# Experts' rows added to the tokens' in DRAM by accumulating scatters

## The chip, the cores and the metric

The kernel runs as one program on one core of a Trainium2 chip. The metric is device time in microseconds, from the start to the end of an execution; lower is better. The engines are named as the profile names them: PE (TensorE, matmul), DVE (VectorE), ACT (ScalarE), POOL (GpSimd, which here also issues the indirect transfers) and SP (SyncE, which issues nearly all loads).

## What is computed

The reference runs two blocks of a network of two layers each over 512 tokens of 1024 numbers. The first block has token mixers and a convolutional feed-forward; the second has token mixing and a mixture of 16 experts. The change is in the mixture of experts. Each token goes to two experts; their results, weighted by gates, are added, and the layer norm takes the sum with the scaled input:

```python
def run_block(args):
    e, toks = args
    xb = x_pad[toks]
    h = jax.nn.silu(xb @ w1[e]) * (xb @ w3[e])
    return h @ w2[e]

yb = lax.map(run_block, (blk_e, slot_tok.reshape(n_blk, MOE_BLOCK)))
y = yb.reshape(-1, D) * slot_gate[:, None]
return jnp.zeros((N + 1, D), x2.dtype).at[slot_tok].add(y)[:N]
...
ffn = moe(x.reshape(B * S, D), w_router, router_bias, w1[l], w3[l], w2[l]).reshape(B, S, D)
x = layer_norm_2(DN_ALPHA_2 * x + ffn, ln2_g[l], ln2_b[l])
```

All is float32. The kernel makes a float32 product of three faster ones: an operand is split into a high and a low part, and hi·hi, lo·hi and hi·lo are added (`mm3`, lines 368 to 370).

## The kernel before

`moe` (called once per layer, about 1810 to 2153 us and 2630 us to the end) first routes: `idx[0]`, the tile `slots`, holds for each expert 96 places (`SLOTS`), in each the row of the token that goes there; a place without a token holds a row beyond the tensor's end and is dropped by the bounds check. `idx[1]`, the tile `slotw`, holds the gates. The token rows lie in DRAM as `xd`. For each expert POOL gathers its rows (`gather`, L1763, `AHEAD` = 4 experts in advance), PE transposes them, `turn` splits them (tile `Txt`), `up` makes 48 matmuls with the weights `wmoeu` (PSUM tile `HP`, result `Ha`), and `down` transposes that, splits it (`Yhi` on ACT, `Ylo` on DVE) and makes two half products c = 0 and 1 of 12 matmuls each with `wmoed` (PSUM tile `YP`). ACT scales the result by the gate into the tile `y` (L1829), and POOL scatters `y` (L1834). The product of expert e - 1 is made beside `up` of expert e; the last expert's, 15, comes after the loop, in the tail.

Before the change the scatters go to `yd`, which has 1024 rows: a token's first expert writes to row t and its second to row 512 + t, so that no row is written twice and the scatters need not wait for each other (the no-dependence group `rows{l}`). The rows of the last expert are set to zero first (`zero`, L1870, and one scatter), since its result never goes to DRAM. In the tail each of the four 128-token parts of h has two loads from `yd` (L1904, into staging tiles `wide`) and two adds, each cut in two halves: columns 0 to 511 on POOL (L1920), the rest on DVE (L1922). The last expert's rows are added on PE: `parts` makes two pieces of the gated result (`both`, L1909 on ACT and L1910 on DVE), and `stats` multiplies them by the one-hot tiles `own` (L1893), after h itself by the identity (L1933, L1935), so that the sum stands in PSUM for the layer norm.

Weights come in pairs of units, 1 MB a load, on SP's queue (`Stream.next`, L2072), into a ring of 6 `wide` tiles and 7 `g8` tiles. In the tail `ds_.apart` makes the splits go to `g8` tiles of their own. `y`, `own`, `zero` and other raw loads share a pool of three 4 KB tiles (`raw`).

Each engine works off its instructions in an order that the framework's scheduler sets before the run; SP's and POOL's queues are in order too, so a transfer that waits holds up those behind it. After layer 0's product PE goes on with the memory branch of the next layer (`memory_whole`, L1495 and L1504), after layer 1's with the final layer norm alone.

Of the kernel before, what the change touches and what calls it, by code (L numbers as in the profile page):

```python
# [21 lines left out]
S = 512  # L22
D = 1024
NT = 4
EPS = 1e-5
ALPHA = math.sqrt(2.0)
# [3 lines left out]
NE = 16  # L30
# [4 lines left out]
SLOTS = 96  # L35
# [253 lines left out]
class Net:  # L289
# [896 lines left out]
    def block2_consts(self):  # L1186
        nc = self.nc
        with self.phase("c2"):
            L = Lane(self, "L", w=8)
            self.tri, self.one_r = (self.blk.tile([128, 128], FR, name=n) for n in ("tri_r", "one_r"))  # L1190
            raw = L.w((128, 128))
            nc.sync.dma_start(raw, self.A["tri"])
            nc.vector.tensor_copy(self.tri, raw)
            nc.vector.tensor_copy(self.one_r, self.ones)
            self.iota = self.const("iota", 128, self.blk)
            self.rcnt = self.const("rcnt", 64, self.blk)
            self.wr = self.const("wr", 128, self.blk)
# [19 lines left out]
            self.yd = self.dram.tile([2 * S, D], F32, name="yd")  # L1217

    def rotary(self, L, ps, bias):

# [523 lines left out]
    def slots(self, L, T, n):  # L1744

        ve = self.nc.vector
        out = self.pp.tile([SLOTS, 2, n], I32, name=self.nm("slots"), tag="slot%d" % n, bufs=1)
        none, second, d = (L.s([SLOTS, n]) for _ in range(3))
        ve.tensor_scalar(none, T, 0.0, 65536.0, op0=OP.is_equal, op1=OP.mult)
        ve.tensor_scalar(second, T, 512.5, -512.0, op0=OP.is_gt, op1=OP.mult)  # L1750
        ve.scalar_tensor_tensor(d, T, -1.0, none, op0=OP.add, op1=OP.add)
        ve.tensor_tensor(out=out[:, 1], in0=d, in1=second, op=OP.add)
        self.placed = ve.tensor_copy(out[:, 0], d)
        return out

    def weights(self, T, n):
# [4 lines left out]
    def gather(self, xg, idx, e):  # L1761

        self.nc.gpsimd.indirect_dma_start(out=xg, out_offset=None, in_=self.xd,  # L1763
                                          in_offset=bass.IndirectOffsetOnAxis(ap=idx[0][:, 1, e:e + 1], axis=0),
                                          bounds_check=S - 1, oob_is_err=False)

    def turn(self, L, xg, raw=False):
# [58 lines left out]
    def rows(self, L, unit, a, idx, e, group=None):  # L1826
# [3 lines left out]
        self.scatter(y, idx, e, group)  # L1830

    def scatter(self, y, idx, e, group=None):

        put = self.nc.gpsimd.indirect_dma_start(out=self.yd,  # L1834
                                           out_offset=bass.IndirectOffsetOnAxis(ap=idx[0][:, 0, e:e + 1], axis=0),
                                           in_=y, in_offset=None, bounds_check=2 * S - 1, oob_is_err=False)
        if group:
            self.tc.declare_no_dep(put.ins, group=group, reason="each pair is one expert's")
            self.tc.add_to_no_dep_group(group, put.ins)

    def moe(self, l, lg, last):
        nc = self.nc
# [5 lines left out]
        def staging():  # L1848
            return self.wide.tile([128, 2, D], F32, tag="wide", bufs=WIDE, name=self.nm("wide"))
# [14 lines left out]
        idx, info = self.route(L, H, l, lg)  # L1864

        self.gather(xg[0], idx, 0)
        self.overflow(L, (T, H, Y), l, info)

        zero = self.rawp.tile([128, D], F32, tag="raw", name=self.nm("zero"))[0:SLOTS]
        with self.tc.issue_after(nc.gpsimd.memset(zero, 0.0).ins):  # L1870
            for e in range(1, AHEAD):
                self.gather(xg[e], idx, e)
            self.scatter(zero, idx, NE - 1, f"rows{l}")
        xt, a = self.turn(T, xg[0]), None
        down = lambda: self.rows(Y, ds_.next, a, idx, e - 1, f"rows{l}")
        unit = lambda: first.pop(0) if first else us.next()
        for e in range(NE):
            nxt = self.up(H, unit, xt, *((down,) if e == NE - 1 else ()))
            if e + 1 < NE:
                xt = self.turn(T, xg[(e + 1) % AHEAD])  # L1880
            if e + AHEAD < NE:
                self.gather(xg[e % AHEAD], idx, e + AHEAD)
            if 0 < e < NE - 1:
                down()
            if 4 <= e < 8:
                with self.tc.issue_after(self.turned.ins):
                    ac.activation(self.h[e - 4], self.h[e - 4], AF.Copy, scale=ALPHA)
            a = nxt
        own = self.rawp.tile([128, NT, 256], FR, tag="raw", name=self.nm("own"))[0:SLOTS, :, 0:128]
        tok = L.s([SLOTS, 1])  # L1890
        ve.tensor_copy(tok, idx[0][:, 1, NE - 1:NE])
        for t in range(NT):
            ve.tensor_scalar(own[:, t], self.iota[0:SLOTS], tok, -128.0 * t, op0=OP.subtract, op1=OP.is_equal)  # L1893
        ds_.apart = True
        last_units = [ds_.next() for _ in range(4)]
        cut = self.cut
        keys = values = None
        if not last:
            keys = self.memory_fetch(l + 1, 0)
        yys = []  # L1900
        for t in range(NT):
            yy = staging()
            for j in range(2):
                nc.sync.dma_start(yy[:, j], self.yd[j * S + t * 128:j * S + (t + 1) * 128, :])  # L1904
            yys.append(yy)
        both = self.g8(FR, (128, 2, D))[0:SLOTS]

        def parts(cs, ps, g):
            ac.activation(both[:, 0, cs], ps, AF.Copy, scale=g)  # L1909
            self.added = ve.scalar_tensor_tensor(both[:, 1, cs], ps, g, both[:, 0, cs].bitcast(F32), op0=OP.mult, op1=OP.subtract)  # L1910

        self.down(Y, iter(last_units).__next__, a, idx, NE - 1, parts)
        product = self.product
        gb = self.ln_rows(6 + 2 * l)
        self.hd = self.dram.tile([S, D], F32, name=self.nm("hd"))
        x = None if last else self.new_x()
        def add(t, after=None):
            z = self.h[t]
            for j in range(2):
                nc.gpsimd.tensor_tensor(out=z[:, 0:512], in0=z[:, 0:512], in1=yys[t][:, j, 0:512], op=OP.add)  # L1920
                with self.tc.issue_after(after.ins) if after else nullcontext():
                    ve.tensor_tensor(out=z[:, 512:D], in0=z[:, 512:D], in1=yys[t][:, j, 512:D], op=OP.add)  # L1922

        rest = staging().rearrange("p a (b c) -> p (a b) c", b=2)
        slots = itertools.count()
        H.w = lambda: rest[:, next(slots) % 4]
# [9 lines left out]
                sums.append(ps)  # L1936
            return self.ln_stats(H, sums)

        add(0, cut)
        add(1, cut)  # L1940
        add(2, self.added)
        fill = iter(())
        if not last:
            self.kv = self.g8()
# [1 line left out]
        with self.tc.issue_after(product.ins):  # L1946
            next(fill, None)
            now = stats(0)
        add(3, self.known_x)
# [11 lines left out]
    def overflow(self, L, lanes, l, info):  # L1961


        nc = self.nc
        ve = nc.vector
        E, g, r, xs, xe, ctr, n = info
        with self.tc.For_i(0, n, 1):
# [43 lines left out]
            self.scatter(y[0], idx, 0, f"rows{l}")  # L2011
            ve.tensor_scalar(ctr, ctr, 1.0, None, op0=OP.add)

    def run(self, upto=99):
# [109 lines left out]
```

## Time and profile before

| | |
|---|---|
| median of 3 runs | 2973.24 us (2969.78 to 2973.51) |
| the profiled execution | 2971.21 us |
| its span | 2969.3 us, so 1.9 us lie around it |
| PE busy | 2864.6 us (96%) |
| DVE busy | 2164.5 us (73%) |
| ACT busy | 1424.0 us (48%) |
| POOL busy | 463.2 us (16%) |
| mean DMA rate | 154 GB/s |

Busy shares are means over stages with different limits. The stage of the change is read by itself: by busy times in a stretch, by the waits of an engine, and in the tails by the timeline, which shows in the order of time what an engine did and what ended its idle time. In a row of the timeline `[1.21 <-DVE Ha L1799]` means 1.21 us idle before it, ended by that instruction. A transfer's time is told as from its issue to its landing.

### The profile page before, as it was taken

To read this page: it belongs to the slowest core of one execution; us is meant where nothing else is said; L and a number is where in the kernel's file an instruction comes from. 1 tells how busy PE (TensorE), PEld (TensorE's weight loads), DVE (VectorE), ACT (ScalarE), POOL (GpSimd) and SP (SyncE) were. 2 spreads that over 40 slices of the span, in tenths; PEclk is the share of its full clock that TensorE was granted. 3 is DMA by queue.
4 is the path that set the end of the run, shared out by engine and by line. 5 is a ranking of instruction groups with operands and counts; after the bars stand their busy time and mean duration, and the time that the engine had idled before them with its cause. 6 is when DMAs were issued, how large, how long until landed. Compare 5 with 4: busy or idle time off the path is not lost.

```text
span 2969.3 us, 37938 instructions
## 1 busy us (share of the span) xinstructions
PE 2864.6 (96%) x13982; PEld 2242.9 (76%) x13982; DVE 2164.5 (73%) x3460; ACT 1424.0 (48%) x2202; POOL 463.2 (16%) x443
## 2 busy tenths in 40 slices
PE   7999999999999999999999998999999999989996
PEld 6777888878678888888777786777687777867774
DVE  6988655665977556677876447999768754479997
ACT  4435433334344333435544424888445444238884
POOL 3412000014221000011101103120412011021203
PEclk9999999999999999999999998999999999989998
DMA  5131333333122333344232266999632322569993
GB/s 193 36 107 37 100 100 96 96 129 95 50 72 76 103 93 101 112 145 125 61 96 82 82 235 237 380 388 367 226 98 61 98 80 82 219 241 370 389 379 123
DMA packets 128589, 457.33 MB, mean 154 GB/s; under 512 B 15696, under 2 KB 16912, under 8 KB 126992
## 3 DMA queue, kind: packets, MB, share of 16 engines
q1 hardware_dynamic: 117776, 425.50, 41.6%
q0 software_dynamic: 7168, 16.79, 1.7%
q10 hardware_dynamic: 3456, 12.58, 1.1%
q8 instruction: 111, 1.82, 0.3%
q14 instruction: 78, 0.64, 0.1%
HBM read 429.12 MB, written 27.26 MB: 154 GB/s over the span
## 4 chain that ended last, share of the span: by engine, by line
PE 66%; DVE 7%; ACT 1%; issue 1%; POOL 1%; DMA 0%; POOLq 0%; DVEq 0%; ACTq 0%
PE AP L368 12%; PE AP L369 12%; PE AP L370 12%; PE HP L370 4%; PE HP L369 4%; PE HP L368 4%; PE YP L370 2%; PE YP L369 2%; PE YP L368 2%; PE BP L370 1%; PE BP L368 1%; PE BP L369 1%; DVE cacc L784 1%; PE O L1610 1%; DVE lo L376 1%
## 5 line engine op out<-in xcount | busy, mean ns | idle before, releaser
L368 PE MATMUL AP<-g,hi 128*128 128x512 f32 (+1 forms) x1856 | 718.1, 388 | 14.1 <-ACT Mw L711 4.0
L369 PE MATMUL AP<-g,hi 128*128 128x512 f32 (+1 forms) x1856 | 711.9, 384 | 8.1 <-DVE g L376 8.1
L370 PE MATMUL AP<-g,lo 128*128 128x512 f32 (+1 forms) x1856 | 712.4, 384 | 0.0
L376 DVE TENSOR_TENSOR lo<-raw,hi 128x1024 fp32r<-128x1024 f32 x314 | 400.2, 1276 | 363.2 <-ACT hi L374 354.2
L374 ACT CAST hi<-raw 128x1024 fp32r<-128x1024 f32 x326 | 341.6, 1050 | 575.6 <-PE AP L369 382.9
L368 PEld LDWEIGHTS AP<-g,hi 128*128 128x128 f32 x1856 | 353.0, 190 | 86.2 <-ACT Mw L711 4.4
L369 PEld LDWEIGHTS AP<-g,hi 128*128 128x128 f32 x1856 | 353.7, 191 | 75.3 <-DVE g L376 9.2
L370 PEld LDWEIGHTS AP<-g,lo 128*128 128x128 f32 x1856 | 353.2, 190 | 67.2 <-issue 2.6
L376 DVE TENSOR_TENSOR lo<-g,hi 128x1024 fp32r<-128x1024 f32 x204 | 239.2, 1219 | 23.4 <-ACT hi L374 23.0
L374 ACT CAST hi<-g 128x1024 fp32r<-128x1024 f32 x204 | 207.0, 1051 | 50.2 <-PE AP L370 32.4
L376 DVE TENSOR_TENSOR lo<-wide,hi 128x1024 fp32r<-128x1024 f32 x180 | 212.4, 1226 | 25.4 <-ACT hi L374 25.2
L370 PE MATMUL HP<-hi,Txt 128*96 128x512 f32 x512 | 203.9, 398 | 0.0
L369 PE MATMUL HP<-lo,Txt 128*96 128x512 f32 x512 | 203.3, 397 | 0.2
L368 PE MATMUL HP<-hi,Txt 128*96 128x512 f32 x512 | 201.0, 400 | 1.1 <-ACT Txt L374 1.1
L374 ACT CAST hi<-wide 128x1024 fp32r<-128x1024 f32 x180 | 182.7, 1050 | 22.2 <-PE HP L370 19.1
L368 PE MATMUL AP<-hi,g 128*128 128x512 f32 x400 | 165.0, 416 | 0.3 <-DVE g L886 0.3
L370 PE MATMUL AP<-hi,g 128*128 128x512 f32 x400 | 157.8, 397 | 0.2 <-DVE g L891 0.2
L369 PE MATMUL AP<-lo,g 128*128 128x512 f32 x400 | 156.8, 393 | 0.0
L368 PE MATMUL BP<-hi,g 128*128 128x512 f32 x352 | 136.8, 390 | 0.0
L369 PE MATMUL BP<-lo,g 128*128 128x512 f32 x352 | 136.6, 389 | 0.0
L370 PE MATMUL BP<-hi,g 128*128 128x512 f32 x352 | 134.1, 389 | 0.0
L384 POOL TENSOR_TENSOR Bs<-Bs,mhalf 128x1 f32<-128x1 f32 x8 | 7.8, 977 | 687.2 <-DVE Bs L383 687.2
(511 smaller groups left out, 5059.1 us busy)
## 6 DMA issues: line engine op xcount, KB each, us to landing
wide<-in_wmoeu SPq DMA_DIRECT2D x64, 1024.0 KB, 7.9
g<-in_wmoeu SPq DMA_DIRECT2D x64, 1024.0 KB, 8.4
raw<-in_wup SPq DMA_DIRECT2D x88, 512.0 KB, 3.5
g<-in_wmoed SPq DMA_DIRECT2D x34, 1024.0 KB, 8.7
wide<-in_wmoed SPq DMA_DIRECT2D x30, 1024.0 KB, 7.9
raw<-in_xwin SPq DMA_DIRECT2D x50, 512.0 KB, 3.6
raw<-in_xgate SPq DMA_DIRECT2D x48, 512.0 KB, 3.6
raw<-in_wdown SPq DMA_DIRECT2D x44, 512.0 KB, 3.5
```

What stands on the lines that cost most here:

```text
L368: mm(ps, a[0], b[0], start=start, stop=False)
L369: mm(ps, a[0], b[1], start=False, stop=False)
L370: self.product = mm(ps, a[1], b[0], start=False, stop=stop)
L374: self.nc.scalar.copy(hi, src)
L376: self.cut = (engine or self.nc.vector).tensor_tensor(out=lo, in0=src, in1=hi.bitcast(F32), op=OP.subtract)
L384: self.nc.gpsimd.tensor_tensor(out=r, in0=x, in1=self.mhalf[:, 0:n], op=OP.pow)
L784: ve.scalar_tensor_tensor(acc, ubs[c][:, j:j + S], w_dw[:, 31 * c + j:31 * c + j + 1], acc, op0=OP.mult, op1=OP.add)
L1610: nc.tensor.matmul(O[j][64 * b:64 * b + 64, t * 128:(t + 1) * 128], v[:, s, c:c + 64], PT[i - 1 + b][:, s, :], start=s == 0, stop=s == t, ...
```

## The change

`yd` is gone. Each layer has a tensor `sums` of 512 rows in DRAM, which starts as the scaled h, and the scatters of experts 0 to 14 add to it in DRAM. Since they go to the same rows, the framework has each wait for the one before. The tail loads four parts from `sums` straight into new h tiles, and no adds are left. The `slots` tile keeps one row number a place instead of two. The scaling of h moves from experts 4 to 7 to before the overflow loop (which runs zero times here), with four writes to `sums` on ACT's queue; `own` moves from the tail to just after that loop. Of the last expert's four weight units, two are split in advance and two when `down` asks for them. The order of POOL's adds and their places (`cut`, `added`) go with the adds.

```diff
     def slots(self, L, T, n):
...
-        ve.tensor_tensor(out=out[:, 1], in0=d, in1=second, op=OP.add)
-        self.placed = ve.tensor_copy(out[:, 0], d)
+        ve.tensor_tensor(out=out, in0=d, in1=second, op=OP.add)
...
+    def scatter(self, y, idx, e):
+
+        self.nc.gpsimd.indirect_dma_start(out=self.sums,
+                                          out_offset=bass.IndirectOffsetOnAxis(ap=idx[0][:, e:e + 1], axis=0),
+                                          in_=y, in_offset=None, bounds_check=S - 1, oob_is_err=False,
+                                          compute_op=OP.add)
...
         self.gather(xg[0], idx, 0)
+
+        self.sums = self.dram.tile([S, D], F32, name=self.nm("sums"))
+        for t in range(NT):
+            ac.activation(self.h[t], self.h[t], AF.Copy, scale=ALPHA)
+            ac.dma_start(out=self.sums[t * 128:(t + 1) * 128, :], in_=self.h[t])
+        mark = info[5]
         self.overflow(L, (T, H, Y), l, info)
-
-        zero = self.rawp.tile([128, D], F32, tag="raw", name=self.nm("zero"))[0:SLOTS]
-        with self.tc.issue_after(nc.gpsimd.memset(zero, 0.0).ins):
+        with self.tc.issue_after(nc.gpsimd.memset(mark, 0.0).ins):
             for e in range(1, AHEAD):
                 self.gather(xg[e], idx, e)
-            self.scatter(zero, idx, NE - 1, f"rows{l}")
+
+        own = self.pp.tile([SLOTS, NT, 128], FR, tag="own", bufs=1, name=self.nm("own"))
...
-            if 4 <= e < 8:
-                with self.tc.issue_after(self.turned.ins):
-                    ac.activation(self.h[e - 4], self.h[e - 4], AF.Copy, scale=ALPHA)
             a = nxt
-        own = self.rawp.tile([128, NT, 256], FR, tag="raw", name=self.nm("own"))[0:SLOTS, :, 0:128]
...
         ds_.apart = True
-        last_units = [ds_.next() for _ in range(4)]
-        cut = self.cut
+        last_units = [ds_.next() for _ in range(2)]
         keys = values = None
         if not last:
             keys = self.memory_fetch(l + 1, 0)
-        yys = []
+        self.new_h()
         for t in range(NT):
-            yy = staging()
-            for j in range(2):
-                nc.sync.dma_start(yy[:, j], self.yd[j * S + t * 128:j * S + (t + 1) * 128, :])
-            yys.append(yy)
+            nc.sync.dma_start(self.h[t], self.sums[t * 128:(t + 1) * 128, :])
...
-        self.down(Y, iter(last_units).__next__, a, idx, NE - 1, parts)
+        self.down(Y, lambda: last_units.pop(0) if last_units else ds_.next(), a, idx, NE - 1, parts)
...
-        def add(t, after=None):
-            z = self.h[t]
-            for j in range(2):
-                nc.gpsimd.tensor_tensor(out=z[:, 0:512], in0=z[:, 0:512], in1=yys[t][:, j, 0:512], op=OP.add)
-                with self.tc.issue_after(after.ins) if after else nullcontext():
-                    ve.tensor_tensor(out=z[:, 512:D], in0=z[:, 512:D], in1=yys[t][:, j, 512:D], op=OP.add)
```

What this does to the order of the instructions is shown at four places. SP's queue in the tail of layer 1 before: the last loads of weights, the loads of `yd`, the layer norm's rows (in brackets the semaphores that an instruction waits on; DMASW counts POOL's transfers, DMAHW those of SP and ACT).

```order
L2072 DMA wide_25390<-in_wmoeu 128x2x1024 [waits DMAHW5_49,DVE_49]
L2072 DMA wide_25423<-in_wmoed 128x2x1024 [waits DMAHW6_49,DVE_49]
L2072 DMA wide_25431<-in_wmoed 128x2x1024 [waits DMAHW7_49,DVE_49]
L1904 DMA wide_25439<-yd 128x1024 [waits DMAHW0_49,DMASW3_49,DVE_49]
L1904 DMA wide_25439<-yd 128x1024 [waits DMAHW1_49]
```

The same place after; between the two pairs of `in_wmoed` stand the four loads of `sums`.

```order
L2054 DMA wide_25372<-in_wmoeu 128x2x1024 [waits DMAHW1_49,DVE_49]
L2054 DMA wide_25398<-in_wmoed 128x2x1024 [waits DMAHW2_49,DVE_49]
L1898 DMA g_25406<-sums_22535 128x1024 [waits DMAHW3_49,DMASW1_49]
L1898 DMA g_25406<-sums_22535 128x1024 [waits DMAHW4_49]
L1898 DMA g_25407<-sums_22535 128x1024 [waits DMAHW5_49,DMASW7_49,PE_49]
L1898 DMA g_25407<-sums_22535 128x1024 [waits DMAHW6_49]
L2054 DMA wide_25438<-in_wmoed 128x2x1024 [waits DMAHW7_49,DVE_49]
```

The first load of `sums` waits on DMASW1, the last scatter's landing; the second pair has moved behind it. DVE before, at the end of the last `up` of layer 1 (`Ha` is its result, `lo` are splits in the ring, `g` splits of the last expert's units):

```order
L376 TENSOR_TENSOR lo_25403<-wide_25390,hi_25402 128x1024
L376 TENSOR_TENSOR g_25425<-wide_25423,g_25425 128x1024
L376 TENSOR_TENSOR g_25428<-wide_25423,g_25428 128x1024
L1799 TENSOR_TENSOR Ha_25412<-HP_25262,Ha_25412 96x512
L376 TENSOR_TENSOR g_25433<-wide_25431,g_25433 128x1024
L1893 TENSOR_SCALAR own_25416<-c_iota,Ls_5398_25417 96x128 x4
L376 TENSOR_TENSOR g_25436<-wide_25431,g_25436 128x1024
L1816 SCALAR_TENSOR_TENSOR Ylo_25458<-YP_25452,Yhi_25457 128x384
L1922 TENSOR_TENSOR g_21914<-g_21914,wide_25439 128x512 x2
```

DVE after, at the same place:

```order
L376 TENSOR_TENSOR lo_25375<-wide_25372,hi_25374 128x1024
L376 TENSOR_TENSOR lo_25385<-wide_25372,hi_25384 128x1024
L1797 TENSOR_TENSOR Ha_25394<-HP_25244,Ha_25394 96x512
L1814 SCALAR_TENSOR_TENSOR Ylo_25419<-YP_25413,Yhi_25418 128x384
L1903 SCALAR_TENSOR_TENSOR g_25412<-YP_25422,slotw_22525,g_25412 96x512
```

Nothing stands between `Ha` and `Ylo` any more: the early pair is split further ahead, the late pair after `parts` of the first half, and `own` at the stage's start. PE in the tail of layer 1 after, where the second half product (`YP_25437`) begins; before, its twelve matmuls stood in a row behind the first half's, and the statistics (L1933, L1935) behind those.

```order
L370 MATMUL YP_25422<-g_25403,Ylo_25419 96x512
L368 MATMUL YP_25437<-g_25440,Yhi_25418 96x512
L1919 MATMUL YP_25508<-g_25407,c_ident 128x512
L1921 MATMUL YP_25508<-g_25412,own_22738 128x512 x2
L1919 MATMUL YP_25512<-g_25407,c_ident 128x512
L369 MATMUL YP_25437<-g_25440,Yhi_25418 96x512
```

Four matmuls of the statistics of part 2 have moved between the first matmul of the second half, which waits for ACT's cast `g_25440` of the late pair, and the second, which waits for its split on DVE. ACT after, in the last two `up` of layer 1 (`y_24842`, `y_25012` and `y_25182` are the rows of experts 11, 12 and 13):

```order
L374 CAST hi_25205<-g_25193 128x1024
L1827 ACTIVATE y_24842<-YP_24852,slotw_22525 96x512
L1827 ACTIVATE y_24842<-YP_24876,slotw_22525 96x512
L374 CAST hi_25219<-g_25217 128x1024
L374 CAST hi_25229<-g_25217 128x1024
L1813 ACTIVATE Yhi_25188<-YP_25183 128x384
L374 CAST g_25400<-wide_25398 128x1024
L374 CAST g_25403<-wide_25398 128x1024
L374 CAST hi_25247<-g_25245 128x1024
L1827 ACTIVATE y_25012<-YP_25022,slotw_22525 96x512
L1827 ACTIVATE y_25012<-YP_25046,slotw_22525 96x512
L374 CAST hi_25257<-g_25245 128x1024
```

And ACT before, where the casts of the same weights stand (`hi_25223` there is `hi_25205` here), with the rows of expert 13 alone:

```order
L374 CAST hi_25223<-g_25211 128x1024
L374 CAST Txt_25185<-TP_25186 128x384
L374 CAST Txt_25185<-TP_25193 128x384
L374 CAST hi_25237<-g_25235 128x1024
L374 CAST hi_25247<-g_25235 128x1024
L1829 ACTIVATE y_25200<-YP_25210,slotw_22550 96x512
L374 CAST hi_25265<-g_25263 128x1024
```

The rows of experts 11 and 12 were made 36 and 18 us ahead of those of 13 before; they have moved to just ahead of them. POOL's order is not shown: it has the gathers and scatters in nearly their old sequence (some gathers one place earlier), each scatter with a further wait on a DMASW semaphore, and the 8 adds of each tail are gone.

## Rows read from the trace of the kernel before

**Rows 1.** Busy time by stretch: us, PE, PEld, DVE, ACT, POOL, clock, DMA, GB/s.

```profile
1860.00:2072.00 212.00, 212.00 (x1008) 150.86 (x1007) 196.90 (x204) 181.03 (x221) 29.40 (x20) 1.00 1.01 381
...
1824.00:1828.00 4.00, 4.00 (x14) 2.65 (x13) 1.11 (x2) 1.44 (x3) 3.04 (x4) 0.55 0.92 356
...
2116.00:2153.00 37.00, 37.00 (x124) 23.07 (x122) 28.49 (x42) 10.10 (x15) 20.42 (x17) 1.00 0.66 233
2929.00:2937.00 8.00, 6.69 (x17) 4.25 (x18) 6.54 (x11) 0.76 (x2) 7.38 (x4) 0.57 1.00 388
```

**Rows 2.** Waits of SP's queue, 1820 to 2106: us in total, times, longest.

```profile
SPq L2072 <- DVE lo L376: 211.4, 80, 7.7
```

**Rows 3.** Timeline of POOL, layer 1's tail: start, us, what [idle before].

```profile
2922.02 0.91 POOL L1834 DMA_INDIRECT yd<-y,slots  x1 [9.77 <-ACT y L1829]
```

**Rows 4.** Timeline of SP's queue, layer 1's tail.

```profile
2889.84 2.86 SPq L2072 DMA_DIRECT2D wide<-in_wmoed  x2
2925.69 4.58 SPq L1904 DMA_DIRECT2D wide<-yd  x8
```

**Rows 5.** Timeline of PE, layer 1's tail.

```profile
2928.00 0.55 PE L1808 MATMUL YP<-c_ident,Ha 96*128 96x96 f32 x4 [1.21 <-DVE Ha L1799]
2929.13 0.47 PE L368 MATMUL YP<-g,Yhi 128*96 128x512 f32 x1 [0.58 <-ACT Yhi L1815]
...
2931.52 0.74 PE L370 MATMUL YP<-g,Ylo 128*96 128x512 f32 x1 [1.18 <-DVE Ylo L1816]
...
2936.75 0.48 PE L369 MATMUL YP<-g,Yhi 128*96 128x512 f32 x1
...
2938.46 0.39 PE L370 MATMUL YP<-g,Ylo 128*96 128x512 f32 x1
2938.69 1.02 PE L1933 MATMUL HP<-g,c_ident 128*128 128x512 f32 x2
```

**Rows 6.** Timeline of DVE, layer 1's tail.

```profile
2927.26 0.68 DVE L1799 TENSOR_TENSOR Ha<-HP,Ha 96x512 f32<-96x512 f32 x1
2927.87 1.21 DVE L376 TENSOR_TENSOR g<-wide,g 128x1024 fp32r<-128x1024 f32 x1
2929.00 0.86 DVE L1893 TENSOR_SCALAR own<-c_iota,Ls 96x128 fp32r<-96x128 f32 x4
...
2930.92 0.55 DVE L1816 SCALAR_TENSOR_TENSOR Ylo<-YP,Yhi 128x384 fp32r<-128x384 f32 x1
```

**Rows 7.** Timeline of POOL, layer 0's tail.

```profile
2100.64 0.91 POOL L1834 DMA_INDIRECT yd<-y,slots  x1 [9.76 <-ACT y L1829]
2107.88 13.33 POOL L1920 TENSOR_TENSOR g<-g,wide 128x512 f32<-128x512 f32 x8 [6.33 <-DMA wide<-yd]
```

**Rows 8.** Timeline of all engines, first statistics of layer 1's tail.

```profile
2944.82 0.64 DVE L1922 TENSOR_TENSOR g<-g,wide 128x512 f32<-128x512 f32 x1
...
2945.60 1.02 POOL L384 TENSOR_TENSOR Hs<-Hs,mhalf 128x1 f32<-128x1 f32 x1 [0.81 <-DVE Hs L383]
```

**Rows 9.** Timeline of ACT at the start of layer 0's stage.

```profile
1824.07 0.48 ACT L374 CAST Txt<-TP 128x384 fp32r<-128x384 f32 x1 [16.00 <-PE TP L1774]
```

**Rows 10.** Line 1834, all scatters of the trace: issue to landing.

```profile
DMA to landing us min/median/max: 3.6/7.5/9.0
```

**Rows 11.** Waits at the start of layer 0's stage, 1806 to 1826.

```profile
POOL zero L1870 <- DMA g<-xd,slots: 4.0, 1, 4.0
```

**Rows 12.** DMA issues on the page: count, KB each, us to landing.

```profile
wide<-in_wmoed SPq DMA_DIRECT2D x30, 1024.0 KB, 7.9
```

**Rows 13.** DMA issues, 2885 to 2969.

```profile
wide<-in_wmoed SPq DMA_DIRECT2D x2, 1024.0 KB, 6.8
...
g<-in_ln_rows SPq DMA_DIRECT2D x1, 1024.0 KB, 11.1
```

**Rows 14.** Timeline of PE, layer 0's last product, around its middle.

```profile
2112.30 0.63 PE L370 MATMUL YP<-g,Ylo 128*96 128x512 f32 x2
```

**Rows 15.** Timeline of ACT, expert 13's first half, layer 1.

```profile
2906.32 0.68 ACT L1829 ACTIVATE y<-YP,slotw 96x512 f32<-96x512 f32 x1
```

More of the change, by code (lines that the diff above doesn't have):

```diff
@@ L1216, in block2_consts @@
             self.xd = self.dram.tile([S, D], F32, name="xd")
-            self.yd = self.dram.tile([2 * S, D], F32, name="yd")
     def rotary(self, L, ps, bias):
@@ L1746, in slots @@
         ve = self.nc.vector
-        out = self.pp.tile([SLOTS, 2, n], I32, name=self.nm("slots"), tag="slot%d" % n, bufs=1)
+        out = self.pp.tile([SLOTS, n], I32, name=self.nm("slots"), tag="slot%d" % n, bufs=1)
         none, second, d = (L.s([SLOTS, n]) for _ in range(3))
@@ L1763, in gather @@
         self.nc.gpsimd.indirect_dma_start(out=xg, out_offset=None, in_=self.xd,
-                                          in_offset=bass.IndirectOffsetOnAxis(ap=idx[0][:, 1, e:e + 1], axis=0),
+                                          in_offset=bass.IndirectOffsetOnAxis(ap=idx[0][:, e:e + 1], axis=0),
                                           bounds_check=S - 1, oob_is_err=False)
@@ L1824, in down, with rows @@
             out(slice(c * 512, c * 512 + 512), ps, idx[1][:, e:e + 1])
-    def rows(self, L, unit, a, idx, e, group=None):
+    def rows(self, L, unit, a, idx, e):
         y = self.rawp.tile([128, D], F32, tag="raw", name=self.nm("y"))[0:SLOTS]
         self.down(L, unit, a, idx, e, lambda cs, ps, g: self.nc.scalar.activation(y[:, cs], ps, AF.Copy, scale=g))
[L1830 to L1839, printed above, removed]
+        self.scatter(y, idx, e)
+    def scatter(self, y, idx, e):
[3 more added lines that the diff above has]
+                                          compute_op=OP.add)
     def moe(self, l, lg, last):
@@ L1866, in moe @@
         self.gather(xg[0], idx, 0)
+        self.sums = self.dram.tile([S, D], F32, name=self.nm("sums"))
[3 more added lines that the diff above has]
+        mark = info[5]
         self.overflow(L, (T, H, Y), l, info)
-        zero = self.rawp.tile([128, D], F32, tag="raw", name=self.nm("zero"))[0:SLOTS]
-        with self.tc.issue_after(nc.gpsimd.memset(zero, 0.0).ins):
+        with self.tc.issue_after(nc.gpsimd.memset(mark, 0.0).ins):
             for e in range(1, AHEAD):
                 self.gather(xg[e], idx, e)
-            self.scatter(zero, idx, NE - 1, f"rows{l}")
+        own = self.pp.tile([SLOTS, NT, 128], FR, tag="own", bufs=1, name=self.nm("own"))
+        tok = L.s([SLOTS, 1])
+        ve.tensor_copy(tok, idx[0][:, NE - 1:NE])
+        for t in range(NT):
+            ve.tensor_scalar(own[:, t], self.iota[0:SLOTS], tok, -128.0 * t, op0=OP.subtract, op1=OP.is_equal)
         xt, a = self.turn(T, xg[0]), None
-        down = lambda: self.rows(Y, ds_.next, a, idx, e - 1, f"rows{l}")
+        down = lambda: self.rows(Y, ds_.next, a, idx, e - 1)
         unit = lambda: first.pop(0) if first else us.next()
@@ L1884, in moe @@
                 down()
-            if 4 <= e < 8:
-                with self.tc.issue_after(self.turned.ins):
-                    ac.activation(self.h[e - 4], self.h[e - 4], AF.Copy, scale=ALPHA)
             a = nxt
-        own = self.rawp.tile([128, NT, 256], FR, tag="raw", name=self.nm("own"))[0:SLOTS, :, 0:128]
[L1890 to L1893, printed above, removed]
         ds_.apart = True
-        last_units = [ds_.next() for _ in range(4)]
-        cut = self.cut
+        last_units = [ds_.next() for _ in range(2)]
         keys = values = None
@@ L1909, in parts @@
             ac.activation(both[:, 0, cs], ps, AF.Copy, scale=g)
-            self.added = ve.scalar_tensor_tensor(both[:, 1, cs], ps, g, both[:, 0, cs].bitcast(F32), op0=OP.mult, op1=OP.subtract)
-        self.down(Y, iter(last_units).__next__, a, idx, NE - 1, parts)
+            ve.scalar_tensor_tensor(both[:, 1, cs], ps, g, both[:, 0, cs].bitcast(F32), op0=OP.mult, op1=OP.subtract)
+        self.down(Y, lambda: last_units.pop(0) if last_units else ds_.next(), a, idx, NE - 1, parts)
         product = self.product
@@ L1937, in stats @@
             return self.ln_stats(H, sums)
-        add(0, cut)
-        add(1, cut)
-        add(2, self.added)
         fill = iter(())
@@ L1948, in moe @@
             now = stats(0)
-        add(3, self.known_x)
         for t in range(NT):
@@ L2010, in overflow @@
             self.down(Y, lambda: (ds_.raw(),), a, idx, 0, out, True)
-            self.scatter(y[0], idx, 0, f"rows{l}")
+            self.scatter(y[0], idx, 0)
             ve.tensor_scalar(ctr, ctr, 1.0, None, op0=OP.add)
```

## The prediction, made before the changed kernel was timed

> **What bounds the kernel now.** I began with the busy times by stretch. In [rows 1] PE is busy for all of 212 us of layer 0's expert loop, DVE for 197 and ACT for 181 of them. The 1008 matmuls are 84 an expert (48 of `up`, 24 of `down`, 12 transposes): 12 experts, 17.7 us each. The DMA share there reads 1.01, but that does not make the DMA the bound: SP, which issues every weight load, spent 211.4 us of the stage waiting for DVE to give a buffer back [rows 2], so loads are asked for when compute lets them be. What the change does inside the stage is free unless it stops PE; the places to read are the two tails, where PE has gaps.
>
> Layer 1's tail in the timeline: expert 14's scatter starts at 2922.02 [rows 3], the first load of `yd` at 2925.69, 3.67 later [rows 4]. PE finishes the last `up` near 2926.8 (2928.00 less 1.21) and waits three times, for Ha, Yhi and Ylo [rows 5]. DVE is why: between Ha and Ylo it does a split, the four `own` rows and another split [rows 6]. PE runs the last product from 2931.52 to 2938.69: the first 13 matmuls follow each other by 0.43 us (2931.52 to 2936.75, twelve steps), the rest by 0.24. The granted clock over 2929 to 2937 is 0.57 [rows 1], so partly at the 1.2 GHz level, after idle times of 1.21, 0.58 and 1.18 us. From 2938.69 to the end of the span are 30.6 us of statistics, layer norm and stores. Layer 0's tail is alike 820 us earlier, but after the product PE has other work (the next block's memory fill) and is busy for 37 of the 37 us to 2153, at a clock of 1.00 [rows 1]. There PE alone sets the end.
>
> **What is removed, at what gain.** The adds on POOL (13.33 us in layer 0 [rows 7], beside PE) end after the product. In layer 1 DVE adds stand between the first statistics and what follows them, one of 0.64 in front of the 1.02 us pow on POOL [rows 8]: I take 0.7 us off layer 1's tail, and nothing off layer 0's, whose path is PE. A split of 1.21, `own` (0.86) and a split like the first go from between Ha and Ylo, and Ha no longer stands behind two splits of the last unit (it began at 2927.26, PE was done at 2926.8: 0.45). Ylo then comes after Yhi alone: Yhi's end (about 2929.1, PE's next start, less 0.45) and 0.55 for Ylo give 2929.2 against 2931.47. So the first half of the last product is 2.3 us earlier in either layer. If nothing else were late, this would be the gain.
>
> **What is moved at no cost.** The scaling of h (8 of about 1 us on ACT) goes from the loop to the stage's start, with four writes on ACT's queue. ACT is idle there for 16.00 us during routing and the first gather [rows 9], so four fit, and the 2 MB of writes have until the first scatter, over 30 us later. `own` (five small DVE instructions, about 1 us) falls behind the first gather's landing, where PE transposes and ACT's Txt come first. If that cover fails, the price is 1 us per layer. The zero scatter and its memset leave POOL, on which nobody waits there.
>
> **What is added: a landing wait, and a load behind it.** Each scatter now waits on POOL for the landing of the one before. In the loop the scatters are 17.7 us apart and landed in 7.5 (median) to 9.0 us [rows 10], so that wait is over before y is there; the gathers queued behind it are for experts two to four ahead and have the same slack. The tail is another matter. Only one of the two 1 MB pairs of the last expert's `w2` stands ahead of the loads of `sums`; SP issues the other behind four loads that wait for expert 14's scatter to land. Before, both went out at 2889.84 [rows 4], 36 us before the scatter landed. So the second half of the last product is late, by a sum of rows with one unknown: L, from an accumulating scatter's start to its landing.
>
> No row shows an accumulating scatter. From below, L is bounded by the plain scatter on idle queues, 3.6 us [rows 10]: it writes the same rows and must read them too, so less is excluded. From above, by a plain scatter with a read in front of it; the nearest read of rows is the first gather, whose waiter stood 4.0 us after its issue [rows 11]: 3.6 + 4.0 = 7.6. Neither row is clearly nearer, so I take the middle, 5.6. The Trainium skill, "Collectives: The Full Stack", section "Stop ④ — SDMA + CCE: where bytes move and the add happens", puts the add into the DMA datapath as the bytes stream through, "with the add free in between"; by it L would be at the lower end, and the sum some 4 us smaller. No run here shows it yet.
>
> Layer 1: the scatter starts at 2922.0 as before (y(14) needs the same matmuls) and lands at 2927.6. SP takes 4.58/8 = 0.57 a load, so the pair goes out at 2930.0. A 1 MB load took 7.9 us [rows 12] (6.8 in the emptier stretch, 11.1 behind eight `yd` loads [rows 13]): landed 2937.9, and after ACT's cast of about 1.0, 2938.9. PE then has 16 matmuls: 12 of the half product and 4 of the statistics that the order puts between. It has stood since about 2931.6, and after shorter gaps it ran 13 matmuls at 0.43 [rows 5]; the same again is 13 x 0.43 + 3 x 0.24 = 6.3, product end 2945.2 against 2938.7: +6.5, less the 0.7: **+5.8**.
>
> Layer 0: scatter 2100.64 [rows 7], landing 2106.2, pair issued 2108.6, landed 2116.5, cast done 2117.5. The first half ended near 2112.5 [rows 14], now 2110.2, so PE idles 7.3 us. Before, PE was at this point at 2112.5 with two of the other twelve matmuls done: 2117.5 - 2112.5 + 2 x 0.24 = 5.5, and with PE busy until 2153 nothing gives it back. The clock comes on top: when PE came out of the wait at the stage's start, the first 4 us were granted 0.55 [rows 1]; 4 us hold some nine matmuls at 0.43, each 0.2 longer, about 2.0: **+7.5**.
>
> Sum +13.3 us on 2971.21, the profiled execution's time (span 2969.3 and 1.9 around it): 2984.5. The median of the runs is 2.0 above that execution, so against it 2986.5; I predict between the two, **2985**. At L = 3.6 both tails are 2 us shorter (+9.3). Above L = 5.3 the chain of scatters begins to count: ACT now makes y(11) and y(12) only about where y(13) stood, 2906.32 [rows 15]. Four scatters must go from there, and three landings fit into 2922 - 2906 = 16 us only up to 5.3. At 7.6 the last lands at 2906 + 4 x 7.6 = 2936.4, 8.8 later than in my sum: about +31 with both tails.
>
> **The rivals.** (a) *The work removed wins.* If the pair did not set the second half, 2.3 us per layer of the earlier Ylo and 0.7 of the adds stay: -5.3, about 2967. For it: 2 MB less to load per tail. Against: the order has the pair behind a wait, and a load of 7.9 us isn't hidden by 2.4 us of matmuls. Chance 0.10. (b) *It cancels:* L near 3.6, the pair landing in 6.8, the clock staying up in both tails: 4 + 2.2 + 4.6 less, about +2.5, 2976. Chance 0.17. (c) *A slow accumulate.* Its place is the chain from y(11) to the loads of `sums`; it decides from L = 5.3 on, with 4 us per tail for each further us. At L = 9.0, the longest plain landing [rows 10], the last lands at 2906 + 36 = 2942 against 2927.6: 13.3 + 2 x 14.4 = +42, 3013. For it: a DMA share of 1.01 in the loop, and a read added to each scatter. Against: in the tail the queues are nearly idle. Chance 0.18. The Trainium skill, "DMA: Bandwidth & Descriptors", section "Rules for kernel authors", has an accumulating DMA wait for the semaphore of an earlier one on the same bytes, since a write that lands in between is lost; by it this chain can't be loosened as that of `yd` was, and it speaks against the change. The order has these waits; no row shows their length. (d) *My forecast:* the late pair, with L between 3.6 and 7.6: 2979 to 3003. Chance 0.55.
>
> **How the numbers follow.** A difference under 0.2%, 6 us, can't be told from none here. Faster is (a) and a little of (b): 0.12. Within 6 us of 2973: most of (b) and the low edge of (d): 0.20. Slower: the rest of (d), and (c): 0.68. The range, 2969 to 3008, leaves out most of (a) and the upper half of (c).
>
> **What would show it.** Right: in both tails SP's last `wide<-in_wmoed` starts 2 to 3 us after the first load of `sums`, PE's longest wait there is for ACT's cast of that pair, 5 to 9 us, and a 212 us stretch of the loop keeps its 1008 matmuls. The landing of the last scatters gives L; scatters that start 5 us or more after y was ready show (c). Wrong: PE idle inside the loop (the accumulates load the queues, or ACT waits for a y buffer), or a pair that lands before the first half is done. Then the sum is made at the wrong place.

## The result

The changed kernel takes 3020.32 us (median of 4 runs, 3016.52 to 3024.37) against 2973.38 us for the kernel before on the same chip (median of 4): a ratio of 1.0164, 95% interval 1.0152 to 1.0176. It is slower by 47 us, where 12 were forecast; the time lies outside the range that was given.

The profiled execution has a span of 3014.5 us, 45.2 more than before. To see where they are I cut each program at the same five points: the start of the first gather of either layer, the end of the last expert's `up` on PE (the start of the transposes of `Ha`, less the idle time before them), and the end of the span. These are the rows of the changed kernel that give the cuts, from the timelines of POOL and PE (start, us, what, idle time before and what ended it):

```profile
1815.40 1.24 POOL L1761 DMA_INDIRECT g<-xd,slots  x1 [13.67 <-DVE slots L1751]
...
2664.35 1.09 POOL L1761 DMA_INDIRECT g<-xd,slots  x1 [14.69 <-DVE slots L1751]
...
2117.30 0.55 PE L1806 MATMUL YP<-c_ident,Ha 96*128 96x96 f32 x4 [0.78 <-DVE Ha L1797]
...
2965.52 0.55 PE L1806 MATMUL YP<-c_ident,Ha 96*128 96x96 f32 x4 [0.78 <-DVE Ha L1797]
```

The same rows before, but for layer 1's transposes, which are in [rows 5] (2928.00 less 1.21):

```profile
1817.71 1.24 POOL L1763 DMA_INDIRECT g<-xd,slots  x1 [13.68 <-DVE slots L1753]
...
2638.14 1.10 POOL L1763 DMA_INDIRECT g<-xd,slots  x1 [13.39 <-DVE slots L1753]
...
2106.62 0.55 PE L1808 MATMUL YP<-c_ident,Ha 96*128 96x96 f32 x4 [1.21 <-DVE Ha L1799]
```

All runs are cut in this way below; "tail 0" goes on through the next block to layer 1's first gather, in which no other part of the program changes.

| us | span | loop 0 | tail 0 | loop 1 | tail 1 |
|---|---|---|---|---|---|
| before | 2969.3 | 287.7 | 532.7 | 288.7 | 42.5 |
| changed | 3014.5 | 301.1 | 547.8 | 300.4 | 49.8 |
| difference | +45.2 | +13.4 | +15.1 | +11.7 | +7.3 |

The rest, -2.3, lies before layer 0's first gather. So there are two causes. One is in the tails, where it was looked for; the other, 25 us, is in the loops, which the prediction held to be free.

**The tails** are as foreseen in kind. SP's queue in both tails:

```profile
2122.54 1.75 SPq L1898 DMA_DIRECT2D g<-sums  x4
2124.34 0.47 SPq L2054 DMA_DIRECT2D wide<-in_wmoed  x1
...
2965.92 1.76 SPq L1898 DMA_DIRECT2D g<-sums  x4
2967.77 0.38 SPq L2054 DMA_DIRECT2D wide<-in_wmoed  x1
```

The late pair goes out 1.8 us after the first load of `sums`, and PE waits for the cast of it, 12.47 and 7.88 us:

```profile
2134.06 0.74 PE L368 MATMUL YP<-g,Yhi 128*96 128x512 f32 x1 [12.47 <-ACT g L374]
...
2977.69 0.74 PE L368 MATMUL YP<-g,Yhi 128*96 128x512 f32 x1 [7.88 <-ACT g L374]
```

The last two scatters of layer 1 on POOL, and the landings of all 30 scatters of the line:

```profile
2951.66 2.11 POOL L1832 DMA_INDIRECT sums<-y,slots  x1 [4.51 <-ACT hi L374]
2960.41 1.57 POOL L1832 DMA_INDIRECT sums<-y,slots  x1 [6.63 <-ACT y L1827]
```

```profile
L1832 POOL DMA_INDIRECT sums<-y,slots x30: 1404/1444/2315, 1857.7 to 2960.4; - x30
...
DMA to landing us min/median/max: 5.4/8.7/9.5
```

The last starts 38.4 us later than before [rows 3], and its landing, 5.5 us later, lets SP go on at 2965.92. The wait before it is for y, not for the chain. In layer 0 the last scatter does wait for the chain. Its y on ACT, and the last two scatters on POOL:

```profile
2111.45 0.70 ACT L1827 ACTIVATE y<-YP,slotw 96x512 f32<-96x512 f32 x1
```

```profile
2108.43 1.41 POOL L1832 DMA_INDIRECT sums<-y,slots  x1 [8.25 <-ACT y L1827]
2114.44 2.31 POOL L1832 DMA_INDIRECT sums<-y,slots  x1 [4.61 <-ACT hi L374]
```

y is done at 2112.15 and the scatter starts 2.3 us later, where a scatter that waits for y alone starts 0.3 after it (2959.45 + 0.69 and 2960.41 in layer 1). The instruction that its row names is not what it waited for: by the trace's semaphore updates the scatter ahead of it landed at 2113.67. So the chain delays the last scatter of layer 0, and the late pair behind it, by 2.0 us. The scatter at 2951.66 waits in the same way, but the one behind it waits longer for its y.

**The loops.** Up to about 2038 us the changed kernel's loop is that of before. Busy time by stretch (columns as in [rows 1]):

```profile
1878.00:1918.00 40.00, 40.00 (x190) 28.46 (x189) 37.46 (x40) 33.61 (x41) 7.01 (x4) 1.00 1.01 368
...
2038.00:2058.00 20.00, 18.25 (x85) 12.52 (x84) 16.28 (x16) 14.67 (x18) 1.40 (x1) 1.00 0.99 400
2058.00:2078.00 20.00, 17.34 (x79) 11.42 (x78) 16.88 (x19) 13.62 (x18) 0.00 (x0) 1.00 0.99 357
2078.00:2098.00 20.00, 13.47 (x53) 8.34 (x53) 12.28 (x14) 12.17 (x16) 1.63 (x1) 0.91 0.28 79
```

In the last four experts PE is idle, 11 us of 60, and DVE and ACT are too. Before, PE was busy for 59.8 of the 60 us at this place:

```profile
2060.00:2080.00 20.00, 19.91 (x94) 13.75 (x93) 18.52 (x19) 16.53 (x21) 0.91 (x1) 1.00 0.76 282
2080.00:2100.00 20.00, 19.88 (x89) 13.61 (x88) 18.69 (x20) 16.31 (x21) 1.19 (x1) 1.00 0.57 199
```

The timeline of PE after:

```profile
2068.90 0.48 PE L369 MATMUL HP<-lo,Txt 128*96 128x512 f32 x1 [1.13 <-DVE lo L376]
...
2072.69 0.47 PE L369 MATMUL HP<-lo,Txt 128*96 128x512 f32 x1 [0.77 <-DVE lo L376]
...
2076.48 0.47 PE L369 MATMUL HP<-lo,Txt 128*96 128x512 f32 x1 [0.76 <-DVE lo L376]
...
2080.27 0.47 PE L369 MATMUL HP<-lo,Txt 128*96 128x512 f32 x1 [0.76 <-DVE lo L376]
...
2085.52 0.47 PE L368 MATMUL YP<-hi,Yhi 128*96 128x512 f32 x1 [2.47 <-ACT y L1827]
...
2091.40 0.74 PE L368 MATMUL YP<-hi,Yhi 128*96 128x512 f32 x1 [2.53 <-DVE Ylo L1814]
```

Twelve matmuls, two units of weights, take 3.79 us instead of 12 x 0.23 = 2.8: PE waits for a split on DVE. DVE waits for the cast on ACT, and ACT for PE, over the same 60 us (waits of ACT: us in total, times, longest):

```profile
ACT hi L374 <- PE HP L370: 11.3, 14, 2.3
ACT hi L374 <- PE YP L370: 6.7, 5, 4.3
```

That is a closed ring: ACT may not cast the next unit until PE has used one of the four places in which splits lie. In the order of the program after the change, the second half product of an expert's `down` stands on PE behind all 48 matmuls of the next `up`, while ACT and DVE make its two splits ahead of that `up`'s. Two of the four places are then held for the whole `up`. For expert 12's `down` and expert 14's `up` in layer 1, PE's order before is: 12 matmuls of the first half, 7 of the second, 1 of `up`, the other 5 of the second, and the rest of `up`. After, it is: 12 of the first half, all 48 of `up`, and then the 12 of the second half. The larger waits, 2.47 and 2.53, come from the same moves: y is made late, so `down` has no place in PSUM for its next half, and a `down` with no `up` beside it waits openly for Ylo. No wait of PE, DVE or ACT in either loop is for the landing of a scatter or of a gather: only POOL waits for these, so it is the order that the three engines pay for.

### The profile page after: what moved, and what is told of

Its sections match the earlier page's. It is cut to its first block, busy times and chain, and to the rows that moved or that the text cites. A ratio compares the mean times of both kernels' runs of the same rounds, so it can differ in the third digit from the quotient of the medians.

```text
span 3014.5 us, 37853 instructions
## 1 busy us (share of the span) xinstructions
PE 2868.6 (95%) x13982; PEld 2242.3 (74%) x13982; DVE 2155.1 (71%) x3442; ACT 1427.6 (47%) x2202; POOL 439.6 (15%) x425
## 5 line engine op out<-in xcount | busy, mean ns | idle before, releaser
L369 PEld LDWEIGHTS HP<-lo,Txt 128*96 128x96 f32 x512 | 83.0, 162 | 50.3 <-DVE lo L376 16.9
```

The lines of the kernel that those rows point to most:

```text
L369: mm(ps, a[0], b[1], start=False, stop=False)
```

## The experiments

My theory after these traces: the chain of waits moves the last experts' work in the order, and that costs the loops 25 us; the late pair costs the tails 22; accumulating itself costs little. Against it stands what the prediction had as its rival (c), that the accumulates are slow or load the queues. "Back" is against the changed kernel, 3020.3.

### Plain writes in the same order

```diff
-                                          in_=y, in_offset=None, bounds_check=S - 1, oob_is_err=False,
-                                          compute_op=OP.add)
+                                          in_=y, in_offset=None, bounds_check=S - 1, oob_is_err=False)
```

> The changed kernel with plain writes in place of accumulating ones, to the same rows, with the same chain of waits; every instruction keeps its place on every engine. Left out: the adding, so a row keeps the last expert that wrote it. Theory 1 (the order costs: with the chain of waits PE's, ACT's and DVE's work of the last experts is put in another order, and in the trace of the changed kernel PE idles 12 us in each loop; the late pair costs the rest): the time stays at 3010 to 3020, at most 4 us per layer below the changed kernel for a shorter landing in the tail. Theory 2 (the accumulate itself costs, by longer landings or by load on the queues): most of the 47 us comes back, 2975 to 2990.

Measured: 3017.56 us, 1.0157 of before (1.0137 to 1.0176). Loops of 300.7 and 303.1, tails of 544.4 and 47.6. The landings of this kernel's scatters:

```profile
L1832 POOL DMA_INDIRECT sums<-y,slots x30: 910/939/1995, 1863.5 to 2965.5; - x30
...
DMA to landing us min/median/max: 3.6/8.0/8.8
```

The accumulate's own price is therefore 1.8 us of landing on idle queues, 0.7 on loaded ones and 0.5 us of POOL for each issue; in the tails that makes 3.4 and 2.2 us. In the loops it makes none that can be seen: one is 0.4 shorter without it and the other 2.7 longer. The order of the instructions is the same, so a loop of a single traced execution is good to some 3 us. Nearly all of the 47 us is there without it, so rival (c) has fallen as their cause.

### The pair ahead of the sums

```diff
+        ds_.fetch(1)
         self.new_h()
         for t in range(NT):
             nc.sync.dma_start(self.h[t], self.sums[t * 128:(t + 1) * 128, :])
```

(`fetch` only loads the pair; `down` has it split when it asks for it.)

> The changed kernel with the last pair of weights loaded ahead of the loads of sums instead of behind them. Theory 1: PE's waits for ACT's cast of that pair (12.5 us in layer 0, 7.9 in layer 1 in the changed kernel's trace) go, with what follows from the clock: 16 to 24 us less than the changed kernel, 2996 to 3004; the loops still idle 12 us each. Rival (the tail then waits for the loads of sums instead, which still stand behind the last scatter): under 8 us less, above 3012.

Measured: 3011.37 us, 1.0140 (1.0121 to 1.0158), only 9 back. The expectation was missed, though the tails did what it said: 539.6 and 42.2, which is 8.2 and 7.6 less. But the loops grew by 3.9 and 3.8, to 305.0 and 304.2: with one load moved the order of the last experts differs once more, and PE's waits in layer 0 from 2038 to 2130 are, among others,

```profile
PE HP L369 <- DVE lo L376: 5.7, 7, 1.1
PE YP L368 <- ACT y L1827: 3.9, 2, 2.5
PE YP L368 <- DVE Ylo L1814: 2.5, 1, 2.5
```

The waits for y are 1.4 us more than the changed kernel's one of 2.47; the rest of the 3.9 I can't place, and it is near what two executions of one order differ by. So the price of the moved order may change even with edits that have nothing to do with the loop.

### Two chains, pair late and pair early

```diff
         self.sums = self.dram.tile([S, D], F32, name=self.nm("sums"))
+        self.odd = self.dram.tile([S, D], F32, name=self.nm("odd"))
...
             ac.dma_start(out=self.sums[t * 128:(t + 1) * 128, :], in_=self.h[t])
+            ac.dma_start(out=self.odd[t * 128:(t + 1) * 128, :], in_=self.h[t])
...
-        self.nc.gpsimd.indirect_dma_start(out=self.sums,
+        self.nc.gpsimd.indirect_dma_start(out=self.odd if e % 2 else self.sums,
```

> The changed kernel with two tensors of sums, one for the even and one for the odd experts, so that a scatter waits for the one two experts earlier; the order of PE's, ACT's and DVE's work in the loop is then that of the kernel before, the pair is still late. Left out: the sums of the odd experts aren't loaded, so their rows are missing from the result; the second tensor adds four writes of 512 KB per layer at the stage's start. Theory 1: the 25 us of the two loops come back and the tails keep their wait: 2988 to 2998. Theory 2 (the accumulates' traffic or landings cost in the loop): at least 3010. By the recorded sum for the late pair alone: 2985.

Measured: 2986.69 us, 1.0058 (1.0040 to 1.0077), 1.3 below the range of theory 1 and near the recorded sum. The loops are 287.9 and 288.6, those of the kernel before; the tails keep their wait, 542.3 and 48.9. Accumulating scatters run in both loops, and PE has no gap in 212 us of them, as in [rows 1]:

```profile
1860.00:2072.00 212.00, 212.00 (x1009) 151.00 (x1008) 198.09 (x205) 178.04 (x216) 33.64 (x20) 1.00 1.02 373
```

This is the kernel that the prediction described: late pair, untouched loops. Its recorded sum was +7.5 and +5.8 for the tails, measured are +9.6 and +6.4; PE's gaps at the pair are

```profile
2115.34 0.74 PE L368 MATMUL YP<-g,Yhi 128*96 128x512 f32 x1 [6.97 <-ACT g L374]
...
2945.17 0.74 PE L368 MATMUL YP<-g,Yhi 128*96 128x512 f32 x1 [4.39 <-ACT g L374]
```

against 7.3 in the sum for either layer (in layer 1 from 2931.6 to 2938.9). With the pair ahead as well:

> As the run with two tensors of sums, and the last pair loaded ahead of the loads of sums. Left out as there: the odd experts' rows. Theory 1: both causes are gone and all that remains is accumulating scatters and less work in the tail: 2966 to 2976, the kernel before or a little less. Theory 2: 2985 or more, since the accumulates are still there.

Measured: 2975.97 us, 1.0016 (1.0007 to 1.0026): loops of 288.4 and 288.0, tails of 535.6 and 44.1. Both causes are gone, and 44 of the 47 us with them. It is at the upper end of what was expected. What the tails keep, 2.9 and 1.6 us, is seen in the timeline of PE in layer 1:

```profile
2935.53 0.39 PE L370 MATMUL YP<-g,Ylo 128*96 128x512 f32 x1
2937.63 0.47 PE L368 MATMUL YP<-g,Yhi 128*96 128x512 f32 x1 [1.71 <-ACT g L374]
2938.29 1.46 PE L1922 MATMUL YP<-g,c_ident 128*128 128x512 f32 x2 [0.20 <-DMA g<-sums]
2938.83 1.78 PE L1924 MATMUL YP<-g,own 96*128 96x512 f32 x2
```

The first half is early, as forecast, but the cast of the pair stands on ACT behind the first half's result, and the statistics in between take 1.46 and 1.78 for two against 1.02 [rows 5], at a granted clock of 0.72 over 2938 to 2940 and 0.50 over 2940 to 2942.

### The chain alone, in the kernel before

```diff
-        if group:
-            self.tc.declare_no_dep(put.ins, group=group, reason="each pair is one expert's")
-            self.tc.add_to_no_dep_group(group, put.ins)
```

> The kernel before with one thing more: each plain scatter to yd waits for the one before it (the no-dependence group is left out). Nothing accumulates, both pairs of the last expert's weights are early, the adds are there. By the order of the program, PE's and ACT's work of experts 10 to 14 is moved here too, much as in the changed kernel. Theory 1 (the waits reorder the loop, and that costs): 8 to 13 us in each loop, 2988 to 3000. Rival (the order is harmless, and the loops of the changed kernel lose their time to something else in the change): within 4 us of the kernel before.

Measured: 3002.15 us, 1.0101 (1.0084 to 1.0118), with loops of 302.0 and 305.7 and tails of 531.1 and 41.3. Nothing accumulates here and no pair is late; a wait on a scatter is all that is added, and it costs 31 us, a little more than theory 1 said (14.3 and 17.1 in the loops against 8 to 13). PE shows the same rhythm as the changed kernel:

```profile
2091.17 0.47 PE L369 MATMUL HP<-lo,Txt 128*96 128x512 f32 x1 [1.55 <-DVE lo L376]
2094.97 0.48 PE L369 MATMUL HP<-lo,Txt 128*96 128x512 f32 x1 [0.77 <-DVE lo L376]
```

### A place of its own for one split

Does PE idle in the moved order because places are held, or because cast and split follow one another in any case? The control has five `wide` tiles instead of six; the test spends the 8 KB that this frees:

```diff
-WIDE = 6
+WIDE = 5
...
+        elif self.own and self.i % 4 == 0:
+            hi = net.pp.tile([128, 1024], FR, tag="hx", bufs=1, name=net.nm("hi"))
+            lo = net.pp.tile([128, 1024], FR, tag="lx", bufs=1, name=net.nm("lo"))
```

(`self.own` is set for the stream of `down`'s weights; the control has the first two lines alone.)

> The changed kernel with five wide tiles for weights instead of six, which frees 8 KB a partition; a control for the next run. Theory 1 and rival: as the changed kernel, 3010 to 3030, loops of about 301 us.

> As the control with five wide tiles, and the 8 KB go to a place of its own for the split of every expert's fourth down unit, so that in the moved order the waiting down product holds one place of the four-deep ring of splits during an up instead of two. Theory (PE idles in the moved order because only two places are left for the splits of up, so that each pair of units costs 3.79 us instead of 2.8): those waits, about 6 us in each loop, go, and 8 to 14 us come back against the control; PE's waits of 2.5 us for Ylo and for y stay. Rival (PE waits for the sequence of cast and split itself, not for places): the same as the control within 4 us.

Measured: the control 3026.00 us (1.0183, 1.0166 to 1.0200), the test 3010.67 (1.0127, 1.0110 to 1.0144): 15 us back, loops of 304.0 and 303.0 against 295.9 and 294.1. PE's waits in layer 1 from 2846 to the end of its loop, of the control:

```profile
PE HP L369 <- DVE lo L376: 6.1, 7, 1.2
PE YP L368 <- ACT y L1827: 4.3, 2, 2.5
```

and of the test:

```profile
PE YP L368 <- ACT y L1827: 2.5, 1, 2.5
PE HP L369 <- DVE lo L376: 2.2, 3, 1.2
```

The waits for a split went from 6.1 to 2.2: with one place more for the splits of `up` PE waits 3.9 us less for them in this loop, of the 14.4 that the control's loop loses against the kernel before. That bears out the ring of four as one cause, of a good quarter of the loss. The loop got 8.9 us back, though, and the 15 us in all are above the 8 to 14 expected: the order of PE's work in the test is not the control's either, and one of the two waits for y went with it, which the theory had staying. What the rest of the loss is made of (the waits for y and what the shifted `down` leaves uncovered) I did not take apart.

### Two chains and all four units ahead

```diff
-        last_units = [ds_.next() for _ in range(2)]
+        last_units = [ds_.next() for _ in range(4)]
```

> As the run with two tensors of sums, and all four last units loaded and split ahead, as in the kernel before. Left out as there: the odd experts' rows. The run with two tensors and an early pair had loops as short as before, but a tail 2.9 and 1.6 us longer, since PE waited 1.7 us for a cast that stood behind the first half's result and ran statistics at the lower clock between. Theory: with that gone the tails are level with the kernel before or up to 2 us shorter each: 2967 to 2974. Rival (the accumulating scatters leave a cost of their own in the tail): 2975 or more.

Measured: 2973.72 us, 1.0002 (0.9993 to 1.0012), loops of 287.5 and 288.5, tails of 532.9 and 41.8. It can't be told from the kernel before. With both causes away, accumulating in DRAM neither costs nor gains: the 16 adds a layer that it saves were not on the path. This run doesn't load and add the odd experts' sums, so what two tensors cost when both are used is not shown.

### One part alone: own early

```diff
-        own = self.rawp.tile([128, NT, 256], FR, tag="raw", name=self.nm("own"))[0:SLOTS, :, 0:128]
...
+        own = self.pp.tile([SLOTS, NT, 128], FR, tag="own", bufs=1, name=self.nm("own"))
```

(With its five DVE instructions, moved into the kernel before at the place that the change gives them.)

> The kernel before with one part of the change alone: the one-hot tiles own are made at the stage's start instead of in the tail between two splits that Ylo waits behind. Theory: the chain through DVE in the tail gets shorter by own's 0.79 us in each layer, and nothing else moves: 1 to 2 us less, 2969 to 2972, at the edge of what can be told. Rival (the small DVE instructions at the stage's start delay the first splits there): 0 to 2 us more.

Measured: 2969.73 us, 0.9995 (0.9986 to 1.0004). In the direction of the expectation, but not clear of no change. No run here beats the kernel before beyond its interval.

## Why the prediction was wrong

**The sign and the place in the tail were right.** The late pair, its wait for the last scatter, and PE's wait for its cast are in the trace at the places named. L was taken as 5.6 us and is 5.4 at the least, 5.5 for the last of layer 1. The sum for the tails was +13.3; in the kernel where only this happens it is +16.0 (9.6 + 6.4), and that kernel's 2986.69 us is 1.7 from the 2985 that was forecast for the changed one. Some of this closeness is luck. In layer 1 the gap was 4.39 us, not 7.3: the first half ended 2.2 us later than in the sum, with matmuls 0.43 apart, and the cast was done 0.7 earlier. From there to the end of the product PE took 7.6 us (2945.17 to 2952.78), not 6.3, so two errors partly cancel. In layer 0 the term for the clock, 2.0, was too small: the granted clock of that kernel from 2115 to 2121 is 0.50, which makes 3.0.

**In the changed kernel the tails cost 22.4, and most of the surplus is in layer 0.** There the landing of the last scatter took 8.1 us, not 5.6: its issue on POOL took 2.31 us instead of 1.44, and two loads for the next block, issued at 2113.80 and 2115.51, run beside it (no run takes them away). The scatter itself started 2.1 us before `up` ended (2114.44, 2116.5), where it was 4.8 before [rows 7]; 2.0 of these 2.7 us are its wait for the chain. From these two PE's gap is 12.47 instead of 7.3. The DMA issues from 2112 to 2136:

```profile
raw<-in_xwin SPq DMA_DIRECT2D x5, 512.0 KB, 9.3
...
wide<-in_wmoed SPq DMA_DIRECT2D x1, 1024.0 KB, 8.6
...
sums<-y,slots POOLq DMA_INDIRECT x1, 8.1
```

**The step that failed is the loop.** The prediction said that the wait for a landing is over before y is there, so that the loop pays nothing. On the chip that nearly is true. In the changed kernel two scatters of a layer start 0.8 us after the landing ahead of them (experts 8 and 14 in layer 0, 8 and 13 in layer 1), and only layer 0's tail pays for it, with 2.0 us; the runs with two chains show accumulating scatters, with waits, beside an unhindered PE. What was missed is that the wait acts before the program runs. The scheduler that sets the order of each engine answered the chain by moving the last experts' y and half products, and the kernel pays for that order whether or not a scatter is ever late. The prediction had half of it in hand: it quoted ACT's order, with y(11) and y(12) moved by two experts and by one, and used it only for when the scatters could go. It did not ask what PE does meanwhile, did not set PE's order of these experts beside the ring of four splits, and so put the cost of the move at nothing, where it was 25 us. Its own sign of being wrong, PE idle inside the loop, is what came: the changed kernel has 990 matmuls from 1860 to 2072 instead of 1008.

**The rival that came nearest in size was right for another reason.** Rival (c) gave 3013 at its upper price, but by slow landings. The chain of landings delayed one scatter that counted, the last of layer 0, by 2.0 us; in layer 1 the wait ahead of the last scatter was for y, and plain writes in the same order gave 3017.56. The bound of 5.3 us for L, from which (c) was to decide, took y(11) to be made where y(13) stood; on the chip it was done 26 and 24 us before y(14). The sign given for (c) came without (c): the scatters of experts 6, 7 and 8 start 18, 18 and 10 us after their y in either layer, with plain writes as well, and no other engine waits for them.

**The gain of 2.3 us per layer was not found either.** The first half product did end early in the run with two chains and an early pair, but there the second half gave it back: 1.71 us for a cast and statistics at the lower clock. With all four units ahead, which keeps the splits of the second pair in the tail, the tails are level with before to within 0.7 us.

## What to carry to other kernels

When a scheduler sets the order, a new dependency is a change of the order of everything around it: compare the order of the bounding engine for the whole stretch, not only at the instruction that waits, and ask which ring or pool is held longer by it. A chain that needs no tight coupling can be given two targets in turn, so that each link has twice the time; here that took the price out of the loops, but the loads and adds of the second target come on top, and no run here has them. And a load that nobody needs to delay must not stand behind one that waits, in a queue that is worked off in order.

## What the runs showed of the hardware

An accumulating scatter of some 64 rows of 4 KB landed 1.8 us later than a plain one on idle queues (5.4 against 3.6) and 0.7 later on loaded ones (medians 8.7 and 8.0), and took POOL 1.44 us to issue instead of 0.94. The Trainium skill, "Collectives: The Full Stack", section "Stop ④ — SDMA + CCE: where bytes move and the add happens", calls the add free as the bytes stream through, and counts the reads apart from it. The runs can't part the two: the read of the destination and the add took 1.8 us together in a single transfer of this size, and nothing that could be seen in a loop in which they are covered.

The clock fell after short waits inside a busy stretch too. The changed kernel has waits of 2.47 and 2.53 us, to 2085.52 and 2091.40. After the first the granted clock stays at 1.00 from 2086 to 2090; after the second it is 0.50, the 1.2 GHz level, from 2092 to 2094, and 0.95 in the next 2 us (0.91 over 2078 to 2098). After the late pair in layer 0 it is 0.62 over 2134 to 2140, before it is back at 1.00:

```profile
2134.00:2140.00 6.00, 5.94 (x17) 4.88 (x18) 3.50 (x3) 1.91 (x3) 0.00 (x0) 0.62 0.86 333
2140.00:2150.00 10.00, 10.00 (x40) 6.92 (x39) 1.45 (x2) 1.43 (x3) 0.00 (x0) 1.00 0.79 284
```

Six us at 0.62 are 6 x 0.38 = 2.3 us of full speed lost, near the 2.0 that the prediction took for it.
